# Sums of squares of a feed-forward block by one-column matrix products, later parking of recurrent weights, and other tile sizes

## The chip, the cores and the metric

The kernel runs on one core of one Trainium2 chip. The metric is the device time of one execution in microseconds (us); before the change its median over 3 runs is 2185.7 us (2184.69 to 2186.59). Engines: TensorE (PE; its weight loads PEld), VectorE (DVE), ScalarE (ACT), GpSimd (POOL) and SyncE (SP, whose queue issues the DMAs).

## The reference

A trunk of two decoder layers on an input of 512 rows (S) by 1024 features (D), all in float32. Each layer is a half feed-forward block, a mixer, and another half feed-forward block. The mixer of the first layer is attention (stick-breaking heads and dilated windows), that of the second a recurrent time mixing (RWKV-7). The change is about the four feed-forward blocks:

```python
def rms_norm(x, g, eps=NORM_EPS):
    y = x * lax.rsqrt(jnp.mean(x * x, axis=-1, keepdims=True) + eps)
    return y * g

def swiglu(h, w_gate, w_up, w_down):          # 1024 -> 2816 -> 1024
    return (jax.nn.silu(h @ w_gate) * (h @ w_up)) @ w_down

x = x + 0.5 * swiglu(rms_norm(x, ffn_norm), w_gate, w_up, w_down)
```

## The kernel before

**Stages.** The program has six stages in a row: feed-forward block 0, attention, blocks 1 and 2, the recurrence (rwkv), block 3. x stays in SBUF, features on the partitions, as eight chunks of 128x512. A float32 product is made of three: each operand is split into a high part (a CAST on ACT) and a low part (a subtract on VectorE), and `mm3` (L121 by its matmuls) adds high x high, high x low and low x high in PSUM. A matmul has a 128x128 stationary block and 512 moving columns.

**A feed-forward block** (`ffn`, L538) goes through steps, one converted weight of 128x1024 each, in the order of `ffn_steps`: four steps "s" (`first`, 24 matmuls each) for the first 256 hidden features, then five tiles of 512 hidden features. In a tile, gate and up products of half-size blocks are combined so that seven products ("1", "2", "6", "7", "5", "3", "4", in two halves of 12 matmuls) do the work of eight. In between stand the transposes of the previous tile's result (`turn`, L683) and its down products (`down`, added to x at L704). The combined inputs come from `prep` (splits of x times the gain, L569 and L570) and `sums` (L578 to L584, split by L330 and L331), held in `xs`. What is called a block's head below is the stretch around steps "s" and products 1 and 2; a tile's step of 24 matmuls is one weight of a product or of a down step.

**The norm.** The mean of squares is needed when the first 256 features go through Silu. `first(3)` squares x in four ACT operations of 128x1024 (L610), each into a room from `work()`, adds the eight chunks up on GpSimd in seven adds (L614), and multiplies the 128x512 sum, four blocks of it stationary, by one column of ones (L616, four matmuls, eight passes on TensorE). Then Ln, Exp, two Newton operations and two more on VectorE give rstd (L441 to L445, L620), four Silu on ACT (L103) and four products on VectorE (L624) the first tile's result `u`; its transposes and everything from product 6 on need these. `work()` hands out four rooms in turn, to sums, squares, gate and up results and the results p, q, v, r of the products; the copy of product 1 into p (L660) takes the room of the third square.

**PSUM** has three pairs of banks for products ("fp") and two single ones ("fd"). Steps "s" hold two pairs until Silu and L624 have read them, product 1 takes the third; product 2 needs a pair that has been read.

**Weights** come by DMA (SyncE) as raw 128x1024 into slots: four constant ones and, inside a block, six `extra` ones in the rooms wx. `_conv` turns a raw one into parts (adds L292 where products combine weights, CAST L295, subtract L296), three weights ahead. The next load into a slot waits for the subtract that last read it (L201).

**Parks.** During blocks 1 and 2 the weights of the recurrence are converted in advance and stored to DRAM ("parked"): `park_some` is called with each weight and at each fifth call takes one of 37 operations; the first two are for the lora matrices, four conversions each (`park_lora`, small pieces on ACT L263 and VectorE L264), the others plain pairs (L241, L242, store L245). They have rooms of their own, praw and pparts.

**Order.** Each engine executes its instructions in program order; that order and the places of tiles in SBUF are chosen at build time by a scheduler from the dependences, so that a change in one place can move instructions elsewhere.

## Time and profile before

| | before |
|---|---|
| median of 3 runs | 2185.7 us (2184.69 to 2186.59) |
| profiled execution: its time, its span | 2183.23 us, 2181.5 us |
| mean granted TensorE clock | 0.968 of full speed |
| TensorE busy | 2033.7 us, 93% |
| VectorE busy | 1593.5 us, 73% |
| ACT busy | 954.9 us, 44% |
| GpSimd busy | 189.7 us, 9% |
| moved by DMA | 282.38 MB, 129 GB/s |

The busy time is the sum of an engine's instructions in one profiled execution; the span is from its first to its last instruction, and the execution's own time lies 1.7 us above it. A clock of 0.5 is 1.2 GHz, 1.0 is 2.4 GHz. In the timelines below a row joins neighbouring instructions of one line, with its start and length and the idle time before it.

### The profile page before, as it was taken

Reading aid. Unit: us, or ns where it says so; the run is one execution under the profiler, and the core shown is the slowest. Engines: PE = TensorE matmul, PEld = TensorE weight load, DVE = VectorE, ACT = ScalarE, POOL = GpSimd, SP = SyncE. Lnnn points to the kernel's source line nnn. Section 1 sums busy time; section 2 is a strip of 40 time slices with the busy share of each in tenths; the row PEclk is TensorE's granted clock in tenths of the full one; section 3 lists DMA queues with packets and bytes.
Section 4 is the critical chain, followed back from the end, with each engine's and each line's share of the span. In section 5 each row is a group of like instructions: output and inputs, shape, how many; then the busy total and the mean of one; then the engine's idle time right before and its main releaser. Section 6 shows DMA issues by size and latency. Waiting matters only on the chain.

```text
span 2181.5 us, 28736 instructions
## 1 busy us (share of the span) xinstructions
PE 2033.7 (93%) x11303; PEld 1625.8 (75%) x11303; DVE 1593.5 (73%) x1958; ACT 954.9 (44%) x1367; POOL 189.7 (9%) x194
## 2 busy tenths in 40 slices
PE   6799999999986999999799999999878898999998
PEld 5688888776874778888678888777556666788887
DVE  7587885557777977887788888556964557787774
ACT  4343443354345534445444445383624424333342
POOL 1100000211003000000200000112321104000000
PEclk9899999999997999999899999999988998999999
DMA  5232332421122475555355575446633332233321
GB/s 175 70 114 87 107 98 69 132 78 49 54 92 93 156 236 203 186 193 179 117 187 177 172 229 185 162 126 212 196 105 90 98 116 92 87 116 116 97 87 39
DMA packets 219294, 282.38 MB, mean 129 GB/s; under 512 B 45395, under 2 KB 135659, under 8 KB 219160
## 3 DMA queue, kind: packets, MB, share of 16 engines
q1 hardware_dynamic: 217048, 278.46, 40.3%
q10 hardware_dynamic: 2112, 2.10, 0.3%
q8 instruction: 89, 1.46, 0.3%
q14 instruction: 45, 0.37, 0.1%
HBM read 227.76 MB, written 54.59 MB: 129 GB/s over the span
## 4 chain that ended last, share of the span: by engine, by line
PE 76%; DVE 11%; ACT 4%; DMA 3%; issue 3%; POOL 2%; SPq 1%; POOLq 0%; DVEq 0%; ACTq 0%
PE fp L121 36%; PE fd L121 17%; PE am L121 6%; PE rm L121 4%; PE rq L121 2%; DVE parts L296 2%; PE wo L121 2%; PE rr L121 2%; PE fd L683 1%; POOL ssum L614 1%; PE rl L121 1%; DVE const L1582 1%; DVE const L1588 1%; ACT parts L295 1%; DMA const<-in_ffn_w_up_dram 1%
## 5 line engine op out<-in xcount | busy, mean ns | idle before, releaser
L121 PE MATMUL fp<-parts,xs 128*128 128x512 f32 x3744 | 909.2, 398 | 40.0 <-ACT wx L660 27.2
L121 PEld LDWEIGHTS fp<-parts,xs 128*128 128x128 f32 x3744 | 708.0, 191 | 190.1 <-ACT wx L660 28.0
L121 PE MATMUL fd<-act,parts 128*128 128x512 f32 x1728 | 410.7, 391 | 5.7 <-DVE act L331 5.5
L121 PEld LDWEIGHTS fd<-act,parts 128*128 128x128 f32 x1728 | 325.5, 189 | 76.6 <-DVE act L331 8.4
L295 ACT CAST parts<-wx 128x1024 fp32r<-128x1024 f32 x220 | 230.3, 1052 | 327.0 <-PE fp L121 212.5
L295 ACT CAST parts<-const 128x1024 fp32r<-128x1024 f32 (+1 forms) x196 | 202.2, 1033 | 320.0 <-PE fp L121 155.8
L296 DVE TENSOR_TENSOR parts<-const,parts 128x1024 fp32r<-128x1024 f32 (+1 forms) x196 | 236.7, 1211 | 107.9 <-ACT parts L295 107.2
L296 DVE TENSOR_TENSOR parts<-wx,parts 128x1024 fp32r<-128x1024 f32 x220 | 266.6, 1222 | 59.2 <-ACT parts L295 58.8
L704 DVE SCALAR_TENSOR_TENSOR const<-fd,const 128x512 f32<-128x512 f32 x160 | 109.3, 688 | 121.5 <-PE fd L121 121.4
L646 DVE TENSOR_TENSOR wx<-fp,wx 128x1024 f32<-128x1024 f32 x140 | 169.0, 1220 | 18.6 <-PE fp L121 18.6
L121 PE MATMUL am<-xg,parts 128*128 128x512 f32 x384 | 99.4, 410 | 0.0
L121 PE MATMUL fp<-act,parts 128*128 128x512 f32 x384 | 92.5, 394 | 1.5 <-ACT act L330 1.5
L121 PEld LDWEIGHTS am<-xg,parts 128*128 128x128 f32 x384 | 71.9, 191 | 25.6 <-issue 9.9
L121 PEld LDWEIGHTS fp<-act,parts 128*128 128x128 f32 x384 | 71.0, 188 | 16.8 <-ACT act L330 2.5
L412 POOL TENSOR_TENSOR ssum<-ssum,sq 128x512 f32<-128x512 f32 x14 | 23.1, 1647 | 642.3 <-ACT sq L411 641.9
L614 POOL TENSOR_TENSOR ssum<-wx 128x512 f32<-128x512 f32 x4 | 25.6, 6396 | 602.5 <-ACT wx L610 602.5
L103 ACT ACTIVATE wx<-wx,const 128x512 f32<-128x512 f32 x80 | 53.5, 717 | 55.7 <-DVE wx L646 55.3
L683 PE MATMUL fd<-const,wx 128*128 128x128 f32 x352 | 60.1, 281 | 18.0 <-DVE wx L624 17.4
L683 PEld LDWEIGHTS fd<-const,wx 128*128 128x128 f32 x352 | 45.6, 144 | 33.0 <-issue 15.9
L330 ACT CAST act<-fd 128x512 fp32r<-128x512 f32 x88 | 47.9, 587 | 33.8 <-PE fd L683 33.4
L331 DVE TENSOR_TENSOR act<-fd,act 128x512 fp32r<-128x512 f32 x88 | 57.7, 687 | 6.1 <-ACT act L330 6.1
L121 PE MATMUL rm<-xm,parts 128*128 128x512 f32 x252 | 60.8, 394 | 0.0
(296 smaller groups left out, 2395.9 us busy)
## 6 DMA issues: line engine op xcount, KB each, us to landing
parts<-pparts SPq DMA_DIRECT2D x68, 512.0 KB
parts<-parts SPq DMA_DIRECT2D x68, 512.0 KB
wx<-in_ffn_w_gate_dram SPq DMA_DIRECT2D x52, 512.0 KB
wx<-in_ffn_w_down_dram SPq DMA_DIRECT2D x52, 512.0 KB
wx<-in_ffn_w_up_dram SPq DMA_DIRECT2D x48, 512.0 KB
const<-in_ffn_w_down_dram SPq DMA_DIRECT2D x36, 512.0 KB
const<-in_ffn_w_up_dram SPq DMA_DIRECT2D x32, 512.0 KB
const<-in_ffn_w_gate_dram SPq DMA_DIRECT2D x28, 512.0 KB
```

The lines of the kernel that those rows point to most:

```text
L103: ins = nc.scalar.activation(out, in_, func, **kw)
L121: return self.pe(self.nc.tensor.matmul(*args, **kw))
L295: self.nc.scalar.copy(hi[:r, :n], raw[:, :n])
L296: self.nc.vector.tensor_tensor(out=lo[:r, :n], in0=raw[:, :n], in1=hi[:r, :n].bitcast(F32), op=ALU.subtract)
L330: self.nc.scalar.copy(hi, t)
L331: self.nc.vector.tensor_tensor(out=lo, in0=t, in1=hi.bitcast(F32), op=ALU.subtract)
L412: nc.gpsimd.tensor_tensor(out=ssum, in0=ssum, in1=sq, op=ALU.add)
L614: nc.gpsimd.tensor_tensor(out=ssum, in0=in0, in1=sq[:, e], op=ALU.add)
L646: add = lambda out, other, ps=ps: nc.vector.tensor_tensor(out=out, in0=ps, in1=other, op=ALU.add)
L683: nc.tensor.transpose(ps[:, b * P : (b + 1) * P], us[n][b][:, f * P : (f + 1) * P], self.ident)
L704: nc.vector.scalar_tensor_tensor(out=self.x[c], in0=ps, scalar=0.5, in1=self.x[c], op0=ALU.mult, op1=ALU.add)
L1582: ins = nc.vector.tensor_tensor(out=pv, in0=L[:, i, j:, None].to_broadcast([P, n, j]), in1=T[:, i : i + 1, :j].to_broadcast([P, n, j]), op ...
```

## The change

Line numbers of the changed program are some five higher: L616 is now among the matmuls of `mm` (L120), L610 is L612, L660 is L665, L683 is L688, L624 is L629, L292, L295 and L296 are L293, L296 and L297, L103 is L102, L264 is L265. The reduce is L623.

1. Squares by TensorE. Each of the four steps "s" squares its two chunks and multiplies each of the eight 128x128 blocks of squares by a column of ones into its own column of a PSUM bank, 32 products of 128x128 by 128x1 in a block (128 in all, 16 before). A reduce on VectorE adds the eight columns of each row block. GpSimd's 28 adds are gone. The bank of the sums, one of two "fd", is held through the four steps.

```diff
 def first(kk):
     if not kk:
+        live["sum"] = self.bank("fd", 2)[:, : 4 * NCH]
...
+    sq, c = work(), 2 * kk
+    nc.scalar.activation(sq, self.x_all[:, c : c + 2], AF.Square)
+    for e in range(2):
+        for b in range(4):
+            col = 4 * (c + e) + b
+            self.mm(
+                live["sum"][:, col : col + 1], sq[:, e, b * P : (b + 1) * P], self.ones[:, 0:1],
+                start=True, stop=True,
+            )
     if kk < 3:
         return
-    ssum, ps = self.row("ssum", 1), self.bank("fd", 2)
-    for c in range(0, NCH, 2):
-        sq = work()
-        nc.scalar.activation(sq, self.x_all[:, c : c + 2], AF.Square)
-        for e in range(2):
-            in0 = ssum if c else sq[:, 0]
-            if c or e:
-                nc.gpsimd.tensor_tensor(out=ssum, in0=in0, in1=sq[:, e], op=ALU.add)
-    for b in range(4):
-        nc.tensor.matmul(
-            ps[:, b : b + 1], ssum[:, b * P : (b + 1) * P], self.ones[:, 0:1], start=True, stop=True
-        )
-    self.rsqrt(rstd, ps[:, :4], 1.0 / D, EPS, scratch)
+    sums_of = live["sum"].rearrange("p (c b) -> p b c", b=4)
+    nc.vector.tensor_reduce(out=total, in_=sums_of, axis=AX.X, op=ALU.add)
+    self.rsqrt(rstd, total, 1.0 / D, EPS, scratch)
```

2. Parks. The count of calls starts anew in each block; only calls 13 to 90 count, and every fourth takes an operation (19 in each of blocks 1 and 2, 38 for 37 operations). The rooms praw and pparts go: the raw weight lies in a room of `wx` and the parts in a pair of `act` rooms.

```diff
-        if self.park_ops and self.park_turn % self.park_every == 0:
+        if self.park_ops and 12 < self.park_turn <= 90 and self.park_turn % self.park_every == 0:
...
-    t.plan_parks(5)
+    t.plan_parks(4)
```

3. Tiles. Rooms are pairs of their own instead of groups; the four first inputs of steps "s" lie in a tile xa of their own, whose other halves lie in xs, so `prep` splits each of the four chunks in two halves of 256; the extra raw slots are five instead of six; some tiles are rounded up to 1024 instead of 512. In the mixers biases, q and k, hidden rows, k, pa and heads are grouped otherwise, with the same operations; the lora weights of the recurrence have four buffers instead of five.

```diff
-        self.conv_ahead = 3
-        XS, WX, AC = MODE
...
+        self.conv_ahead, self.park_turn = 3, 0
+        room = [self.pair("wx", 10) for _ in range(10)]
+        x1 = self.t("xa", [4, 2, 256], 1, F32R)
+        xs = [(self.t("xb", [2, 2, 256], 4, F32R), self.t("xs", [2, 4, 256], 4, F32R)) for _ in range(4)]
+        act_room, pair = [self.pair("act", 4, F32R) for _ in range(4)], self.t("acts", [2, 2, S], 1, F32R)
+        act_room += [pair[:, e] for e in range(2)]
+        self.park_room = room[-5], pair
-        self.extra = [room[i].rearrange("p e s -> p (e s)") for i in range(6)]
+        self.extra = [room[i].rearrange("p e s -> p (e s)") for i in range(5)]
...
-        for z in range(4, 10):
+        for z in range(4, 9):
             self.slot_last[z] = -1
...
         def prep(c):
-            hi, lo = (xs[c % 4][:, e, 0:4:3] if c < 4 else xs[c % 4][:, e, 1:3] for e in range(2))
             x = halves(turned(c) if turned else self.x[c])
...
+            if c < 4:
+                parts = [((x1[:, c, 0], x1[:, c, 1]), x[:, 0]), ((xs[c][1][:, 0, 0], xs[c][1][:, 1, 0]), x[:, 1])]
+            else:
+                parts = [((xs[c - 4][0][:, 0], xs[c - 4][0][:, 1]), x)]
...
-            t = act_room[next(turns[6]) % 6]
+            t = act_room[(f + 4) % 6 if n == TILES - 1 else f]
...
-            t = self.t("lw", [2, LORA], 5, F32R)
+            t = self.shaped(self.sb.tile([P, 2 * LORA], F32R, tag="lw", name="lw", bufs=4), [2, LORA])
```

What this does to the engines' orders, at three places (block 3's head, block 1's head, block 1's first tile). On TensorE at the head of block 3 (fp: the products' banks, fd: the single banks; xs, xa and xb: inputs; ssum and wx: the summed squares before, a room with squares now), before:

```order
L121 MATMUL fp<-parts,xs 128x512 x98
L616 MATMUL fd<-const,ssum 128x1 x4
L121 MATMUL fp<-parts,xs 128x512 x24
L683 MATMUL fd<-const,wx_12851 128x128 x6
L121 MATMUL fp<-parts,xs 128x512 x18
L683 MATMUL fd<-const,wx_12851 128x128 x2
```

and now:

```order
L120 MATMUL fp<-parts,xb 128x512 x24
L120 MATMUL fd<-const,wx 128x1 x8
L120 MATMUL fp<-parts,xb 128x512 x24
L120 MATMUL fp<-parts,xa 128x512 x10
L120 MATMUL fd<-const,wx 128x1 x8
L120 MATMUL fp<-parts,xa 128x512 x14
L120 MATMUL fp<-parts,xb 128x512 x24
L688 MATMUL fd<-const,wx 128x128 x6
L120 MATMUL fp<-parts,xs 128x512 x12
```

The four products with ones (L616) stood behind all steps "s" and product 1 and ahead of product 2; now eight stand behind each of the last steps and the last eight inside product 1, and product 2 (the x24 before the transposes L688) has none ahead of it at its start.

On ACT at the head of block 1 (L610 and L612: squares; L660 and L665: the copy of product 1; L263: lora parks), before:

```order
L610 ACTIVATE wx_4147<-const 128x1024
L295 CAST parts<-const 128x1024 x2
L330 CAST xs<-wx_4147 128x1024
L610 ACTIVATE wx_4147<-const 128x1024
L263 ACTIVATE pparts<-praw,const 128x64 x4
L263 ACTIVATE pparts<-praw,const 128x160
L263 ACTIVATE pparts<-praw,const 128x32
L263 ACTIVATE pparts<-praw,const 128x128
L610 ACTIVATE wx_4147<-const 128x1024 x2
L660 COPY wx_4147<-fp 128x1024
```

and now, from the third square on:

```order
L612 ACTIVATE wx<-const 128x1024
L296 CAST parts<-wx 128x1024
L331 CAST xs<-wx 128x1024
L296 CAST parts<-const 128x1024
L665 COPY wx<-fp 128x1024
L296 CAST parts<-const 128x1024
L102 ACTIVATE const<-const 128x4 x2
L98 ACT_TABLE_LOAD
L296 CAST parts<-const 128x1024
L296 CAST parts<-wx 128x1024
L102 ACTIVATE wx<-fp,const 128x256 x4
```

The lora pieces are gone from between the squares and the copy; Ln and Exp (L102 on 128x4), the table load and two CASTs of weights stand ahead of the four Silu (L102 on 128x256).

On VectorE at the same place (L441 to L620, now L442 to L625: rstd from the sums; L624 and L629: the first tile's result), before:

```order
L296 TENSOR_TENSOR parts<-const,parts 128x1024
L441 SCALAR_TENSOR_TENSOR const<-fd,const 128x4
L442 SCALAR_TENSOR_TENSOR const<-const 128x4
L445 SCALAR_TENSOR_TENSOR const<-const 128x4
L620 TENSOR_SCALAR const<-const 128x4
L296 TENSOR_TENSOR parts<-wx_4146,parts 128x1024
L624 SCALAR_TENSOR_TENSOR wx_4147<-fp,const,wx_4147 128x256 x4
```

and now:

```order
L623 TENSOR_REDUCE const<-fd 128x4
L297 TENSOR_TENSOR parts<-const,parts 128x1024
L442 SCALAR_TENSOR_TENSOR const<-const 128x4
L293 TENSOR_TENSOR const<-const 128x1024
L293 TENSOR_TENSOR const<-wx,const 128x1024
L443 SCALAR_TENSOR_TENSOR const<-const 128x4
L293 TENSOR_TENSOR wx<-const,wx 128x1024
L446 SCALAR_TENSOR_TENSOR const<-const 128x4
L297 TENSOR_TENSOR parts<-const,parts 128x1024
L625 TENSOR_SCALAR const<-const 128x4
L297 TENSOR_TENSOR parts<-wx,parts 128x1024
L629 SCALAR_TENSOR_TENSOR wx<-fp,const,wx 128x256 x4
```

The four small operations stood side by side; now the reduce stands ahead of them, and three adds of weights (L293) and two subtracts (L297) between.

On VectorE in the first tile of block 1 (L655 and L660: the last operation of products 3 and 4; L331 and L332: splits of a transposed piece; L242 and L264, L265: parks), before:

```order
L292 TENSOR_TENSOR wx_4147<-const,wx_4147 128x1024
L296 TENSOR_TENSOR parts<-const,parts 128x1024
L292 TENSOR_TENSOR const<-const,wx_4146 128x1024
L296 TENSOR_TENSOR parts<-wx_4146,parts 128x1024
L242 TENSOR_TENSOR pparts<-praw,pparts 128x1024
L292 TENSOR_TENSOR const<-wx_4146 128x1024
L296 TENSOR_TENSOR parts<-wx_4146,parts 128x1024
L331 TENSOR_TENSOR act_4149<-fd,act_4149 128x512 x2
```

and now:

```order
L293 TENSOR_TENSOR wx<-wx 128x1024
L297 TENSOR_TENSOR parts<-wx,parts 128x1024 x2
L265 SCALAR_TENSOR_TENSOR acts<-wx,const,acts 128x64 x4
L265 SCALAR_TENSOR_TENSOR acts<-wx,const,acts 128x160
L265 SCALAR_TENSOR_TENSOR acts<-wx,const,acts 128x32
L265 SCALAR_TENSOR_TENSOR acts<-wx,const,acts 128x128
L297 TENSOR_TENSOR parts<-wx,parts 128x1024
L332 TENSOR_TENSOR act<-fd,act 128x512 x2
L293 TENSOR_TENSOR wx<-const,wx 128x1024
L293 TENSOR_TENSOR const<-const,wx 128x1024
L265 SCALAR_TENSOR_TENSOR acts<-wx,const,acts 128x64 x2
L293 TENSOR_TENSOR const<-wx,const 128x1024
```

Where one plain park (L242) stood, a whole lora conversion (the four rows of L265, seven pieces) and the beginning of the next stand now; all eight lora conversions lie in this tile, six of them ahead of the second pair of splits (L332).

## Rows read from the trace of the kernel before

**Rows 1.** Page, part 1: engine, busy us (share of span), instructions.

```profile
PE 2033.7 (93%) x11303; PEld 1625.8 (75%) x11303; DVE 1593.5 (73%) x1958; ACT 954.9 (44%) x1367; POOL 189.7 (9%) x194
```

**Rows 2.** Stretches (us): each engine's busy time, granted clock, DMA share, GB/s.

```profile
100.00:300.00 200.00, 199.14 (x901) 164.44 (x900) 160.81 (x163) 79.12 (x87) 0.00 (x0) 1.00 0.35 106
740.00:780.00 40.00, 32.92 (x139) 25.76 (x138) 34.34 (x40) 19.49 (x28) 0.00 (x0) 0.91 0.59 199
1120.00:1140.00 20.00, 17.89 (x79) 14.15 (x78) 20.00 (x21) 10.60 (x13) 0.00 (x0) 0.91 0.63 209
```

**Rows 3.** Waits: engine, line, awaited, us in all, times, longest.

```profile
ACT wx L660 <- POOL ssum L614: 26.1, 4, 7.9
```

**Rows 4.** Timeline, TensorE, four block heads: start, us, instructions [idle before].

```profile
63.95 7.03 PE L121 MATMUL fp<-parts,xs 128*128 128x512 f32 x22 [12.53 <-ACT wx L660]
...
78.16 2.05 PE L121 MATMUL fp<-parts,xs 128*128 128x512 f32 x4
...
686.84 7.85 PE L121 MATMUL fp<-parts,xs 128*128 128x512 f32 x22 [14.64 <-ACT wx L660]
694.52 0.95 PE L616 MATMUL fd<-const,ssum 128*128 128x1 f32 x8
...
703.18 1.11 PE L683 MATMUL fd<-const,wx 128*128 128x128 f32 x4 [0.28 <-DVE wx L624]
703.95 2.33 PE L121 MATMUL fp<-parts,xs 128*128 128x512 f32 x5
...
1066.93 1.87 PE L616 MATMUL fd<-const,ssum 128*128 128x1 f32 x8 [7.75 <-POOL ssum L614]
...
1075.62 2.73 PE L121 MATMUL fp<-parts,xs 128*128 128x512 f32 x6
...
1845.85 1.87 PE L616 MATMUL fd<-const,ssum 128*128 128x1 f32 x8 [8.95 <-POOL ssum L614]
...
1858.96 3.59 PE L121 MATMUL fp<-parts,xs 128*128 128x512 f32 x9
```

**Rows 5.** Timeline, GpSimd, block 1's head.

```profile
679.48 9.91 POOL L614 TENSOR_TENSOR ssum<-ssum,wx 128x512 f32<-128x512 f32 x6
```

**Rows 6.** Timeline, ACT, heads of blocks 0 and 1.

```profile
55.49 2.00 ACT L610 ACTIVATE wx<-const 128x1024 f32<-128x1024 f32 x2
...
675.94 1.88 ACT L263 ACTIVATE pparts<-praw,const 128x64 fp32r<-128x64 f32 x7
677.72 1.99 ACT L610 ACTIVATE wx<-const 128x1024 f32<-128x1024 f32 x2
685.77 1.01 ACT L660 COPY wx<-fp 128x1024 f32<-128x1024 f32 x1 [6.07 <-POOL ssum L614]
...
697.60 0.26 ACT L103 ACTIVATE const<-fd,const 128x4 f32<-128x4 f32 x1
...
698.11 1.28 ACT L99 ACT_TABLE_LOAD   x1
...
700.36 0.83 ACT L103 ACTIVATE wx<-fp,const 128x256 f32<-128x256 f32 x2
```

**Rows 7.** Timeline, VectorE, head of block 0 and first tile of block 1.

```profile
56.88 2.17 DVE L292 TENSOR_TENSOR wx<-const,wx 128x1024 f32<-128x1024 f32 x1
...
75.83 0.87 DVE L624 SCALAR_TENSOR_TENSOR wx<-fp,const,wx 128x256 f32<-128x256 f32 x2
...
736.96 1.60 DVE L264 SCALAR_TENSOR_TENSOR pparts<-praw,const,pparts 128x64 fp32r<-128x64 f32 x7
...
747.76 1.22 DVE L292 TENSOR_TENSOR const<-const 128x1024 f32<-128x1024 f32 x1
```

**Rows 8.** Waits of SyncE's DMA queue.

```profile
SPq L201 <- DVE parts L296: 1047.8, 224, 33.3
SPq L245 <- DVE pparts L242: 172.2, 33, 16.7
```

More of the change, by code (lines that the diff above doesn't have):

```diff
@@ L129, in t @@
         n = math.prod(shape)
-        t = self.sb.tile([P, -(-n // S) * S], dtype, tag=tag, name=tag, bufs=bufs)[:, :n]
+        unit = 2 * S if tag in ("vecs", "ssum", "rstd", "recur") else S
+        t = self.sb.tile([P, -(-n // unit) * unit], dtype, tag=tag, name=tag, bufs=bufs)[:, :n]
         return self.shaped(t, shape)
@@ L495, in plan_ffn @@
         for z in steps:
-            i, every = at[z], range(10)
+            i, every = at[z], range(9)
             if z[0] == "s":
@@ L584, in sums @@
             stt(out=t[:, 3], in0=t[:, 1], scalar=-1.0, in1=y12, op0=ALU.mult, op1=ALU.subtract)
-            self.split(t, xs[k][:, 0, 3:7], xs[k][:, 1, 3:7])
+            self.split(t, xs[k][1][:, 0], xs[k][1][:, 1])
         def x_part(k, block, b):
-            return tuple(xs[k][:, e, block, b * P : (b + 1) * P] for e in range(2))
+            bs = slice(b * P, (b + 1) * P)
+            if not block:
+                return tuple(x1[:, k, e, bs] for e in range(2))
+            t, i = (xs[k][0], block - 1) if block < 3 else (xs[k][1], block - 3)
+            return tuple(t[:, e, i, bs] for e in range(2))
         def first(kk):
             if not kk:
+                live["sum"] = self.bank("fd", 2)[:, : 4 * NCH]
                 live["s"] = [t[:, e] for t in (self.banks2(), self.banks2()) for e in range(2)]
@@ L794, in attn_tables @@
         self.bias = []
+        rooms = [self.t(f"bias{g}", [8, P]) for g in range(2)]
         for g, (off, n, kw) in enumerate(((0, 384, 256), (384, 256, P), (640, 256, P))):
@@ L845, in project_v @@
                     f(b, ps[:, i * 256 : (i + 1) * 256], st["rcol"][:, c : c + 1])
-        qkv = self.t("sb", [3, 2, S])
-        qs, ks, vs = qkv[:, 0], qkv[:, 1], qkv[:, 2].rearrange("p i s -> p (i s)")
+        qs, ks, vs = (self.pair("sb", 3) for _ in range(3))
+        vs = vs.rearrange("p i s -> p (i s)")
         for i in range(4):
@@ L889, in attn @@
             merge(out)
-        qk = {}
+        qk, room = {}, [None]
         def evac_norm(ps, g, which):
-            t = all_qk[:, 2 * g + which, :]
+            if not which:
+                room[0] = self.pair("dqk", 6)
+            t, work = room[0][:, which], self.pair("dsq")
+            sq, y = work[:, 0], work[:, 1]
             nc.vector.tensor_tensor(out=t, in0=ps, in1=st["rstd"], op=ALU.mult)
-            sq = self.row("dsq")
             nc.scalar.activation(sq, t, AF.Square)
@@ L1265, in plane @@
     def plane(self, sg, j, i):
-        return self.rw["heads", sg][:, 4 * j + i if i < 4 else 16 + j].rearrange("p c t -> p (c t)")
+        t = self.rw["heads", sg][:, 4 * j + i] if i < 4 else self.rw["us", sg][:, j]
+        return t.rearrange("p c t -> p (c t)")
     def head_keep(self, n, sg, y):
         plane, r = self.heads_at[n, sg]
-        self.split(y, *(self.hids[r + 32 * e : r + 32 * e + 8, plane, :] for e in range(2)))
+        self.split(y, *(self.hid(plane)[r + 32 * e : r + 32 * e + 8] for e in range(2)))
     def head_spread(self, n, m):
@@ L1321, in evac_k @@
         def evac_k(half, ps):
-            all4 = self.t("k", [4, S], 2)
             for i in range(4):
-                t = k_t[4 * half + i] = all4[:, i, :]
+                if i == 0 and not half:
+                    k_t.append(self.t("k", [8, S]))
+                t = k_t[4 * half + i] = k_t[-1][:, 4 * half + i]
                 nc.scalar.copy(t, ps[i])
@@ L1598, in rw_inverse @@
             nc.sync.dma_start(t0[lo], src)
-        us = rw["heads", sg][:, 16:]
+        us = rw["us", sg]
         for s in (1, 0):
```

71 lines of the change are left out of this document (30 added, 41 removed).

## The prediction

> **What bounds the kernel now.** I read the page first: TensorE is busy 93% of the span and VectorE 73% [rows 1]. So only time in which TensorE stands still, or runs slow, can be won. The table of stretches then shows where that is. In the middle of a block it is nowhere: 100 to 300 us is 199.1 us busy at a granted clock of 1.00, 901 matmuls, 0.221 us each, with VectorE at 80% [rows 2]. The waits name the cause: the COPY of product 1 (L660) waits 26.1 us, four times, for GpSimd's sums of squares (L614) [rows 3]. The four block heads on TensorE's timeline show it in place [rows 4]: idle 12.53 us in block 0 and 14.64 in block 1, both released by that COPY, 7.75 in block 2 and 8.95 in block 3, both released by the sums themselves, 43.9 together. The reader should see in each the stretch from the end of product 1 to the start of product 6 (the row after the transposes):
>
> - block 0: 51.42 (63.95 less 12.53) to 78.16, 26.7 us
> - block 1: 672.20 to 703.95, 31.8 us
> - block 2: from 1059.18, with 22 matmuls of product 2 already done (a free PSUM pair let them go ahead), to 1075.62, 16.4 us
> - block 3: 1836.90 to 1858.96, 22.1 us
>
> TensorE needs of this only 24 x 0.221 = 5.3 us for product 2, 0.95 for eight passes with ones [rows 4] and about 1.1 for six transposes (four took 1.11, and the next matmul begins inside them): 7.4 us, in block 2 2.5 us. So 19 + 24 + 14 + 15 = 72 us are lost at the heads, against a whole idle share of some 148 us. Part of it is slow clock: the eight passes took 0.95 us in block 1 and 1.87 us in blocks 2 and 3, right after a wait; the 22 matmuls after block 1's wait took 7.85 us where 4.9 is their pace [rows 4].
>
> **GpSimd's sum goes.** Seven adds on GpSimd per block; in block 1 the last six took 9.91 us, up to 689.4 [rows 5]. The COPY of product 1, whose room held the third square, waited for them and ended at 686.8 [rows 6]. Afterwards a square is read by eight one-column matmuls and is free. All 28 adds go. VectorE gains a little besides: an add (L292) that took 2.17 us while GpSimd ran is elsewhere 1.22 [rows 7].
>
> **128 small matmuls instead of 16.** Each is two passes. The row of eight passes gives 0.95/8 = 0.119 us a pass at full clock, 0.234 at the lower level [rows 4]. Per block 28 more matmuls are 56 x 0.119 = 6.7 us, 27 us in all; that is the bill if TensorE has nothing to wait for, 52 us if all ran at the low clock, nothing if all fill idle time. In blocks 0 and 1 TensorE waits in the first products for VectorE and ACT anyhow, so I let the first 24 be free there and charge only the last eight (1.9 us). In blocks 2 and 3 product 1 runs without gaps up to its end, so 24 x 0.238 = 5.7 us are charged before it. The Trainium skill (TensorE: Matmul & The Clock Gate, section "Wait — 56ns, not 53.3ns?") states that start-to-start never drops below about 25 ns however small the matmul: by that floor the eight would cost 0.4 us and the 24 before them 1.2, and the time would be 4 x 1.5 + 2 x 4.5 = 15 us lower than I give, 2132. The rows show a pass nearly five times as dear, and the rows decide.
>
> **What stays behind the last square.** VectorE's reduce of 128x32 is not in the trace: not below nothing, and not above the 0.44 of a 128x256 operation (half of the pair of L624 in [rows 7]); I take 0.2, since it is an eighth as long. Then Ln and Exp, 0.51 from the one's start to the table load's, the table load 1.28, two pairs of Silu 0.83 each [rows 6], the last L624 0.44 [rows 7], six transposes 1.1: 5.2 us. In the order of the change two CASTs of 128x1024 stand between table load and Silu, each as the COPY 1.01 [rows 6], so 7.2. In block 1 three adds (L293) stand on VectorE inside the chain, between the small operations, 3 x 1.22 = 3.7 us more [rows 7]: 10.9. Product 2's 5.3 us lie inside that. Now the start of product 6, block by block:
>
> - block 0: the last square ended at 57.5 on ACT; 57.5 [rows 6] + 1.9 + 5.2 to 7.2 = 64.6 to 66.6, I take 65.6 against 78.16: 12.6 us won.
> - block 1: the last square ended at 679.7 [rows 6]; one lora conversion (1.88 us on ACT) stood before it and is moved away, so 677.8 + 1.9 + 10.9 = 690.6 against 703.95: 13.4 won.
> - block 2: product 1 ended about 1059.2 - 4.9 = 1054.3; + 5.7 + 1.9 + 7.2 = 1069.1; I take 1069.6 against 1075.62: 6 won.
> - block 3: 1836.9 + 5.7 + 1.9 + 7.2 = 1851.7; the COPY of product 1 now stands behind Exp and the table load, so product 2 starts some 1.3 us late but still ends in time; 1852 against 1858.96: 7 won.
>
> Together 39.0 us.
>
> **The parks, moved.** Before, lora conversions (1.88 us of ACT [rows 6], 1.60 for seven eighths of the same on VectorE [rows 7]) lay in block 1's head and first tile. Now none starts before the 13th weight of a block, and all eight fall into the first tile of block 1, where VectorE was already the bound: 740 to 780 us has it busy 34.3 of 40 us and TensorE 32.9 [rows 2]. Six of them come before the second pair of transposed splits where four and two plain parks were: 1.4 us more by the difference, 5 us if none finds a hole. I charge 3.5. In block 2 the reverse: 1120 to 1140 had VectorE busy 20.0 of 20 us [rows 2]; fewer parks fall there, 2 to 4 us back, I take 3. Net 0.5 lost.
>
> **Other sizes.** In each block four inputs are split in halves, four more operations on each of ACT and VectorE, 16 in all. One cannot cost more than a 128x256 row, 0.44 [rows 7], nor less than nothing: 0 to 7 us on each engine, under ACT's and VectorE's waits for the input at a block's start. I take zero, and 7 us if that cover is gone. The rounding and the pairs move tiles only; the instructions on them stay, and I put them at zero, with plus or minus 5 us for attention and rwkv, whose order on TensorE hardly moves. A raw slot is lost: see the rival.
>
> **Sum.** 39.0 - 0.5 = 38.5. The profiled execution took 2183.2 us (span 2181.5) and the runs' median is 2185.7, 2.5 above. So 2183.2 - 38.5 + 2.5 = **2147 us**. A measurement here can tell about 0.2%, 4.4 us.
>
> **Rivals.**
> 1. *The small matmuls lie on the path everywhere.* The first 24 in blocks 0 and 1 cost 11.4 us more, and if the last eight and half of the rest ran at the low clock another 4 x 3 us: 2147 + 23 = 2170. For it: clock low after each wait [rows 4]. Against: those heads wait for ACT and VectorE, not TensorE. Chance 0.15.
> 2. *Slower: weights come late.* Raw slots fall from ten to nine per block, and for two loads in each tile (the second half of product 6 and the second down step) the distance from the freeing of a slot to its next use falls from three steps to two, 24 x 0.221 = 5.3 us a step. SyncE's queue issues loads in order and waits already: 1047.8 us, 224 times, longest 33.3, for the subtract that frees a slot, and 172.2 us, longest 16.7, in front of a park's store [rows 8]; parks now stand closer, every fourth weight. 512 KB at the 209 GB/s of [rows 2] are 2.5 us. Two such loads in a row, with two conversions of 1.01 + 1.22 us and, by my estimate, 3.5 us of queueing, must fit in four steps, 21.2 us: 5 + 4.5 + 3.5 does. It decides from a landing of about 6.6 us. Then 40 loads are late by 1.5 to 3 us: 60 to 120 us, less 38.5, so 2207 to 2267. Only two of the four blocks hold parks; if only those are hit (20 loads), 2177 to 2207. Against it: mid-block losses are nil with a lead of three steps. Chance 0.15, of which 0.11 slower and 0.04 within 0.2%.
> 3. *VectorE takes over in block 1.* All eight lora conversions in one VectorE-bound tile and the reduce's chain queued behind adds in every block: the 1.5 us not yet charged there, and 3.7 us in the three other heads: 2147 + 13 = 2160. Chance 0.15.
> 4. *All 128 are hidden and the clock stays up.* No charge for small matmuls in blocks 2 and 3: 2147 - 11 = 2136, with the five microseconds of other stages 2131. Chance 0.1.
>
> **How the numbers follow.** The forecast has 0.45, on its own 2137 to 2157. The range takes in rivals 1, 3 and 4: 2131 to 2174; beyond it lie rival 2 and little else, less than 0.2. Faster 0.85 (forecast and rivals 1, 3, 4), same 0.04, slower 0.11.
>
> **What would show it.** Right: GpSimd's adds gone; no wait of L665 for GpSimd; product 6 near 66, 691, 1070 and 1852, each less what was won before it (so near 66, 678, 1047 and 1820); 0.119 us a pass; TensorE's idle time down by some 40 us while its busy time rises. Rival 1: busy time up by over 20 us with clock low at the heads. Rival 2: TensorE waiting for CASTs (L296) that wait for loads in mid-tile, over 1 us, at the same two steps of each tile. Rival 3: idle time before matmuls released by VectorE in block 1's first tile above 10 us. I am wrong if a head keeps a gap over 8 us, or if attention or rwkv moves by more than 5.

## The result and the profile after

The changed kernel takes 2153.96 us (median of 4 runs, 2152.94 to 2157.91) beside 2185.19 of the kernel before on the same chip: ratio 0.9861, 95% interval 0.9844 to 0.9878, 31 us less. The forecast was 2147, with a range of 2131 to 2174. The profiled execution has a span of 2152.0 us, 29.5 less than before, at a mean clock of 0.980 (0.968 before).

The page's first part, engine by engine (busy, share, instructions):

```profile
PE 2054.0 (95%) x11527; PEld 1648.2 (77%) x11527; DVE 1586.2 (74%) x1978; ACT 957.1 (44%) x1383; POOL 126.7 (6%) x166
```

Against [rows 1] TensorE is busy 20.3 us more, VectorE 7.3 less, GpSimd 63 less. So TensorE's idle time fell by 50 us, of which 20 went into more busy time: 112 more small products, 224 passes.

The four heads on TensorE's timeline (start, length, instructions, idle before), as in [rows 4]:

```profile
56.39 1.84 PE L120 MATMUL fd<-const,wx 128*128 128x1 f32 x16
61.99 6.84 PE L120 MATMUL fp<-parts,xb 128*128 128x512 f32 x21 [3.77 <-ACT wx L665]
...
70.24 1.98 PE L120 MATMUL fp<-parts,xs 128*128 128x512 f32 x8
...
674.97 1.84 PE L120 MATMUL fd<-const,wx 128*128 128x1 f32 x16
676.67 5.75 PE L120 MATMUL fp<-parts,xb 128*128 128x512 f32 x24
685.29 0.41 PE L688 MATMUL fd<-const,wx 128*128 128x128 f32 x2 [2.88 <-DVE wx L629]
...
686.64 3.84 PE L120 MATMUL fp<-parts,xs 128*128 128x512 f32 x9
...
1038.84 1.84 PE L120 MATMUL fd<-const,wx 128*128 128x1 f32 x16
...
1052.50 3.11 PE L120 MATMUL fp<-parts,xs 128*128 128x512 f32 x13
...
1817.88 1.84 PE L120 MATMUL fd<-const,wx 128*128 128x1 f32 x16
...
1824.16 5.74 PE L120 MATMUL fp<-parts,xb 128*128 128x512 f32 x24 [1.10 <-ACT wx L665]
...
1830.31 3.00 PE L120 MATMUL fp<-parts,xs 128*128 128x512 f32 x12
```

The four long gaps are gone or small: 12.53 us became 3.77 in block 0, 14.64 became 2.88 (behind product 2, not ahead of it), 7.75 and 8.95 became none and 1.10. A run of 16 passes (records of a one-column product on TensorE, two for each product) took 1.84 us in every head, 0.115 a pass, with the clock up. One run is another matter: in block 1 those of the first two steps "s" stand back to back, 32 passes, and the granted clock falls to 0.5 inside it without a wait, so that the run and the 21 large products behind it are slow:

```profile
650.64 4.75 PE L120 MATMUL fd<-const,wx 128*128 128x1 f32 x32
...
655.25 7.15 PE L120 MATMUL fp<-parts,xb 128*128 128x512 f32 x21
```

The large products, down products among them, are as many as before, so the start of the n-th of a block can be compared in both traces (us; product 1 begins with the 97th, product 6 with the 145th). The last column counts from the end of the block before, so that a mixer in between is included:

| | before | after | difference | won |
|---|---|---|---|---|
| block 0, product 1 | 41.5 | 48.6 | +7.1 | |
| block 0, product 6 | 78.2 | 70.2 | -7.9 | |
| block 0, 241st large product | 101.8 | 92.0 | -9.8 | |
| block 0, last product | 391.3 | 385.1 | -6.2 | 6.2 |
| block 1, first product | 639.4 | 633.6 | -5.7 | |
| block 1, product 1 | 666.6 | 669.5 | +2.9 | |
| block 1, product 6 | 703.9 | 686.6 | -17.3 | |
| block 1, last product | 1026.6 | 1010.6 | -16.0 | 9.8 |
| block 2, product 1 | 1048.6 | 1038.2 | -10.4 | |
| block 2, product 6 | 1075.6 | 1052.5 | -23.1 | |
| block 2, last product | 1391.3 | 1368.6 | -22.7 | 6.7 |
| block 3, product 1 | 1831.3 | 1815.6 | -15.7 | |
| block 3, product 6 | 1859.0 | 1830.3 | -28.6 | |
| block 3, last product | 2174.0 | 2144.5 | -29.5 | 6.8 |

Attention and the recurrence win or lose next to nothing (from block 0's end to block 1's start -6.2 to -5.7, from block 2's end to block 3's start -22.7 to -24.0). In every block the steps ahead of product 1 became longer, by 5.6 to 8.6 us, and what follows it up to product 6 shorter by 13 to 20. The 48 passes ahead of product 1 are 5.5 us at 0.115; the rest of the lengthening is 3 us in block 1, where the clock fell, and 1.9 and 2.8 in blocks 0 and 3, where e1 below, without the passes, is 1.3 and 2.7 longer as well.

### The profile page after: what moved, and what is told of

Read it like the earlier page. It is cut to its first block, busy times and chain, and to the rows that moved or that the text cites. A ratio compares the mean times of both kernels' runs of the same rounds, so it can differ in the third digit from the quotient of the medians.

```text
span 2152.0 us, 29193 instructions
## 1 busy us (share of the span) xinstructions
PE 2054.0 (95%) x11527; PEld 1648.2 (77%) x11527; DVE 1586.2 (74%) x1978; ACT 957.1 (44%) x1383; POOL 126.7 (6%) x166
## 4 chain that ended last, share of the span: by engine, by line
PE 76%; DVE 11%; DMA 5%; ACT 3%; issue 3%; SPq 1%; POOL 0%; ACTq 0%; DVEq 0%; POOLq 0%
PE fp L120 36%; PE fd L120 17%; PE am L120 7%; PE rm L120 4%; DVE parts L297 2%; PE rq L120 2%; PE wo L120 2%; PE rr L120 1%; PE rl L120 1%; DVE const L1593 1%; DMA const<-in_ffn_w_up_dram 1%; DVE const L1599 1%; DVE wx L293 1%; ACT parts L296 1%; DMA wx<-in_ffn_w_up_dram 1%
## 5 line engine op out<-in xcount | busy, mean ns | idle before, releaser
L120 PE MATMUL fp<-parts,xs 128*128 128x512 f32 x2016 | 494.2, 395 | 12.2 <-DVE parts L297 6.4
L120 PEld LDWEIGHTS fp<-parts,xs 128*128 128x128 f32 x2016 | 379.4, 189 | 96.0 <-DVE parts L297 9.7
L120 PE MATMUL fd<-act,parts 128*128 128x512 f32 x1728 | 409.0, 390 | 2.2 <-DVE acts L332 1.6
L296 ACT CAST parts<-wx 128x1024 fp32r<-128x1024 f32 x224 | 234.1, 1052 | 347.0 <-PE fp L120 167.3
L120 PEld LDWEIGHTS fd<-act,parts 128*128 128x128 f32 x1728 | 324.2, 188 | 72.4 <-DVE acts L332 3.4
L297 DVE TENSOR_TENSOR parts<-wx,parts 128x1024 fp32r<-128x1024 f32 x224 | 272.6, 1222 | 76.0 <-ACT parts L296 75.7
L296 ACT CAST parts<-const 128x1024 fp32r<-128x1024 f32 (+1 forms) x192 | 198.3, 1033 | 268.6 <-PE fp L120 135.4
L120 PE MATMUL fp<-parts,xb 128*128 128x512 f32 x1152 | 291.3, 401 | 8.7 <-ACT wx L665 4.9
L297 DVE TENSOR_TENSOR parts<-const,parts 128x1024 fp32r<-128x1024 f32 (+1 forms) x192 | 230.0, 1199 | 73.3 <-ACT parts L296 68.3
L120 PEld LDWEIGHTS fp<-parts,xb 128*128 128x128 f32 x1152 | 216.8, 191 | 55.3 <-ACT wx L665 5.4
L120 PE MATMUL fp<-parts,xa 128*128 128x512 f32 x576 | 141.8, 395 | 2.1 <-ACT xa L569 2.1
L120 PEld LDWEIGHTS fp<-parts,xa 128*128 128x128 f32 x576 | 108.6, 190 | 25.7 <-ACT xa L569 2.5
L120 PE MATMUL am<-xg,parts 128*128 128x512 f32 x384 | 99.5, 411 | 0.0
L120 PEld LDWEIGHTS am<-xg,parts 128*128 128x128 f32 x384 | 72.0, 191 | 25.5 <-issue 10.1
L102 ACT ACTIVATE wx<-wx,const 128x512 f32<-128x512 f32 x80 | 53.5, 717 | 43.1 <-DVE wx L651 42.7
L242 ACT CAST acts<-wx 128x1024 fp32r<-128x1024 f32 (+2 forms) x37 | 37.1, 1003 | 63.3 <-DMA wx<-in_rw_wk_dram 19.1
L120 PE MATMUL rm<-xm,parts 128*128 128x512 f32 x252 | 60.9, 395 | 0.0
L331 ACT CAST act<-fd 128x512 fp32r<-128x512 f32 x80 | 43.6, 587 | 35.3 <-PE fd L688 35.2
L243 DVE TENSOR_TENSOR acts<-wx,acts 128x1024 fp32r<-128x1024 f32 (+2 forms) x37 | 43.1, 1164 | 20.1 <-ACT acts L242 20.0
```

Source lines behind the costliest of these rows:

```text
L102: ins = nc.scalar.activation(out, in_, func, **kw)
L120: return self.pe(self.nc.tensor.matmul(*args, **kw))
L242: nc.scalar.copy(hi, src)
L243: nc.vector.tensor_tensor(out=lo, in0=src, in1=hi.bitcast(F32), op=ALU.subtract)
L296: self.nc.scalar.copy(hi[:r, :n], raw[:, :n])
L297: self.nc.vector.tensor_tensor(out=lo[:r, :n], in0=raw[:, :n], in1=hi[:r, :n].bitcast(F32), op=ALU.subtract)
```

## The experiments

Each kernel ran beside the kernel before on its chip; kernels on different chips are compared by their ratios to it, and a difference in us is that of the ratios times 2183. The changed kernel stands at 0.9861.

Theory A: the gain is the squares' way off GpSimd, and nothing else. Theory B: the later parks carry a part. Theory C: the tile sizes do. Four kernels take parts of the change away or double one.

**e1, all but the squares.**

```diff
-            nc.vector.tensor_reduce(out=total, in_=sums_of, axis=AX.X, op=ALU.add)
...
+                        nc.gpsimd.tensor_tensor(out=ssum, in0=in0, in1=sq[:, e], op=ALU.add)
...
+                nc.tensor.matmul(
+                    ps[:, b : b + 1], ssum[:, b * P : (b + 1) * P], self.ones[:, 0:1], start=True, stop=True
+                )
```

> The changed kernel with the squares summed on GpSimd again (seven adds and four one-column products per block, as before); parks and tile sizes stay changed. Theory A (the gain is the squares' way off GpSimd): about 2185 us, within 5 of the kernel before, and the gaps of TensorE at the four heads are back (over 7 us each, released by the copy of product 1 or by the sums). Theory B (the later parks carry a good part of the gain): 2165 to 2175. Theory C (tile sizes and places carry it): also 2165 to 2175, and the run with sizes alone is then faster than before as well.

Measured: 2187.12 us, ratio to before 1.0026 (1.0013 to 1.0040). The gaps are back, in block 2 half as long as before and in block 1 longer (17.06 us); here on TensorE's timeline in blocks 0, 2 and 3:

```profile
63.92 7.43 PE L120 MATMUL fp<-parts,xb 128*128 128x512 f32 x22 [13.37 <-ACT wx L665]
...
1063.85 1.05 PE L621 MATMUL fd<-const,ssum 128*128 128x1 f32 x8 [3.77 <-POOL ssum L619]
...
1850.65 6.71 PE L120 MATMUL fp<-parts,xb 128*128 128x512 f32 x22 [9.84 <-ACT wx L665]
```

Without the squares nothing is left of the gain; what the other two parts do together costs some 6 us. The squares are worth 36 us. Theory A holds; as sources of the whole gain B and C fall. The edit moves two things at once, the sum from GpSimd to TensorE and the squares from the last step "s" to all four; early squares with GpSimd's sum kept were not run.

**e2, the old rule for parks in the changed kernel.**

```diff
-        if self.park_ops and 12 < self.park_turn <= 90 and self.park_turn % self.park_every == 0:
+        if self.park_ops and self.park_turn % self.park_every == 0:
...
-        self.conv_ahead, self.park_turn = 3, 0
+        self.conv_ahead = 3
...
-    t.plan_parks(4)
+    t.plan_parks(5)
```

> The changed kernel with the old rule for parks: every fifth call from the start of block 1, no window; the rooms they use stay the changed ones. Theory A: 2154 to 2162; the lora conversions lie in the head of block 1 again, which loses 2 to 6 us there, and block 1's first tile and the later tiles of block 2 get 1 to 4 us back. Theory B: 2165 or more. If the closer parks cost more than they win: under 2152.

Measured: 2156.93, ratio 0.9888 (0.9873 to 0.9903), 6 us over the changed kernel (3 by the medians; the two intervals overlap). In e2 and e3 one park falls into block 1's last tile, where its room still holds a transposed piece, so that two down steps compute with other values; the work is the same. Counted between the same products, block 1 ends as in the changed kernel (-16.6 against -16.0) and block 2 as well (-22.1 against -22.7). The difference stands at the end of the recurrence (its last products -17.3 against -20.8). The rule is worth 3 to 6 us, at the edge of what the runs can tell, and not where the forecast looked for it.

**e3, the tile sizes alone** (squares as in e1, parks as in e2).

> Only the tile sizes, rooms, halves of the first inputs and the nine instead of ten raw slots are changed; squares on GpSimd and the old rule for parks. Theory A (sizes are worth nothing): 2181 to 2189. Theory C (sizes win): under 2180. The forecast's rival of late weights (nine slots): over 2190, with waits of TensorE for weights in the middle of the tiles.

Measured: 2191.80, ratio 1.0050 (1.0031 to 1.0070): 9 to 11 us slower. None of it is lost in the middle of block 0's tiles: its last product starts 1.0 us late, product 6 was 0.6 late. It is lost in heads: in block 1 product 2 starts 11.6 us late (1.1 at the block's start), of which 5.4 are left at the block's end (the recurrence takes them back), and in block 3 product 6 comes 4.4 us later than at the block's start. In block 1 the copy of product 1 stands behind a lora conversion on ACT, which waits for the store of the one before it:

```profile
695.62 1.88 ACT L264 ACTIVATE acts<-wx,const 128x64 fp32r<-128x64 f32 x7 [6.35 <-DMA lora<-acts]
```

So the sizes cost about 11 with the old rule, the new rule gives 5 of them back (e3 to e1), and the squares win 36 (e1 to the change) or 35 (e3 to e2). The 5 are at the edge: the intervals of e3 and e1 overlap, and in the two profiled executions 0.7 of them are left (spans of 2187.9 and 2187.2 us), since in e3 the recurrence takes back what block 1's head lost.

**e4, each one-column product twice.**

```diff
                 for b in range(4):
                     col = 4 * (c + e) + b
-                    self.mm(
...
+                    for _ in range(2):
+                        self.mm(
...
```

> The changed kernel with each of its 128 one-column products issued twice in a row, the second with the same result as the first: 32 more per block, 7.6 us of TensorE at 0.119 us a pass and two passes each, 30.5 in all. If they lie on the path in every block: 2180 to 2187. As the forecast charged them (the first 24 free in blocks 0 and 1): 2154 + 4 x 1.9 + 2 x 5.7 = 2173. If they fill idle time: within 4 of 2154. Stage by stage, the distance from the first matmul of a block to product 6 shows it.

Measured: 2201.28, ratio 1.0074 (1.0048 to 1.0101), 46 us over the changed kernel. They lie on the path in all four blocks, but 46 is half as much again as the passes at full clock. TensorE's timeline at the head of block 2, where the changed kernel had its clock at 1.00 throughout (its stretch first, columns as in [rows 2], where the granted clock is the third figure from the end; then e4):

```profile
1010.00:1055.00 45.00, 44.56 (x233) 37.70 (x232) 35.86 (x53) 26.70 (x36) 0.00 (x0) 1.00 0.20 71
```

```profile
1031.11 3.63 PE L120 MATMUL fd<-const,wx 128*128 128x1 f32 x32
...
1040.18 3.83 PE L120 MATMUL fd<-const,wx 128*128 128x1 f32 x32
1043.87 7.13 PE L120 MATMUL fp<-parts,xb 128*128 128x512 f32 x24
1050.84 4.21 PE L120 MATMUL fd<-const,wx 128*128 128x1 f32 x32
1054.91 8.37 PE L120 MATMUL fp<-parts,xb 128*128 128x512 f32 x24
```

Runs of 32 passes now take 3.63 us and more, and the 24 products behind them 7.13 and 8.37 us where 5.75 is their pace. No wait stands ahead of any of them. The stretch of this head is busy without a gap, at a mean clock of 0.88:

```profile
1025.00:1080.00 55.00, 55.00 (x284) 47.34 (x283) 33.08 (x49) 24.96 (x34) 0.00 (x0) 0.88 0.16 57
```

**e8, the same doubled products in runs half as long**, to see whether the length of the run lowers the clock (the lines that these replace are left out).

```diff
...
                 if k >= 4:
                     sums(k - 4)
+                if k % 2 == 0:
+                    sq = work()
+                    nc.scalar.activation(sq, self.x_all[:, k : k + 2], AF.Square)
+                for b in range(4):
+                    for _ in range(2):
+                        self.mm(
+                            live["sum"][:, 4 * k + b : 4 * k + b + 1], sq[:, k % 2, b * P : (b + 1) * P],
+                            self.ones[:, 0:1], start=True, stop=True,
+                        )
...
```

> As e4, each of the 128 one-column products twice, but the 16 products of a step in two groups of 8 (four blocks, twice), each group behind the 12 large products of its own chunk. e4 took 47 us for 128 more products, of which the passes at full clock explain 30: there a run of 32 passes lasted 3.6 us and the granted clock fell to 0.5 within or right after it, with no wait before. Theory (the clock falls because such a run keeps TensorE's array nearly idle): with runs of 16 passes the clock of block 2's head stays at 1.00 and product 6 of block 2 comes 6 us earlier, counted from the block's start, than in e4; time 2180 to 2190. Rival (the doubled products cost more for another reason, as writing the same column twice): as e4, 2198 to 2204.

Measured: 2184.42, ratio 1.0008 (0.9996 to 1.0019), 32 us over the changed kernel, close to the passes alone (30). In block 2's head 12 or 24 large products stand between runs of 1.84 us, and they keep their pace:

```profile
1026.73 1.84 PE L120 MATMUL fd<-const,wx 128*128 128x1 f32 x16
...
1037.56 3.03 PE L120 MATMUL fp<-parts,xb 128*128 128x512 f32 x12
...
1054.13 1.84 PE L120 MATMUL fd<-const,wx 128*128 128x1 f32 x16
1055.83 5.75 PE L120 MATMUL fp<-parts,xa 128*128 128x512 f32 x24
```

The clock of the stretch is 1.00:

```profile
1019.00:1068.00 49.00, 48.70 (x282) 42.13 (x281) 32.81 (x49) 24.89 (x34) 0.00 (x0) 1.00 0.18 62
```

The head of block 2 is 5.6 us shorter than in e4 (from the block's first product to product 6). In block 1 the runs of e8 are not short: 64 passes stand in a row, and there the clock falls as in e4:

```profile
644.67 9.49 PE L120 MATMUL fd<-const,wx 128*128 128x1 f32 x64
```

So the fall of the clock goes with the longer run; writing a column twice cost nothing beyond its passes. The Trainium skill (TensorE: Matmul & The Clock Gate, section "What's actually happening") says that the clock is set by how busy TensorE has been recently. The profile's busy time does not tell it here: in e4's stretch it is 55.00 of 55.00 us at a mean clock of 0.88, so a TensorE that issues one-column products without a break can be granted 1.2 GHz.

**e5, one pass instead of two.** If the passes are on the path, halving them must win.

```diff
-        self.parts_all = self.cp.tile([P, 8192], F32R, name="parts")
+        self.parts_all = self.cp.tile([P, 8194], F32R, name="parts")
...
+        self.one_r = self.parts_all[:, 8192:8194]
+        nc.scalar.copy(self.one_r, self.ones[:, 0:2])
...
-            sq, c = work(), 2 * kk
+            sq, c = act_room[kk], 2 * kk
...
-                        live["sum"][:, col : col + 1], sq[:, e, b * P : (b + 1) * P], self.ones[:, 0:1],
+                        live["sum"][:, 2 * col : 2 * col + 2], sq[:, e, b * P : (b + 1) * P], self.one_r,
```

> The changed kernel with the squares written in the fast float32 form that takes one pass on TensorE instead of two (into act rooms), the moving column doubled to two equal ones: the same 128 products, one pass each, squares rounded a little more. A group of 16 passes took 1.84 us, so 8 passes save 0.92 us a group, 3.7 a block. Theory A (the small products lie on the path in every block): 14.7 us less, 2137 to 2142. The forecast's split (24 of them free in blocks 0 and 1): 4 x 0.9 + 2 x 2.8 = 9.2 less, 2144 to 2147. If they are hidden: within 4 of 2154.

Measured: 2164.14, ratio 0.9915 (0.9900 to 0.9929), 12 us slower than the changed kernel. The expectation missed altogether, and not at the heads: product 6 of block 0 comes 1.7 us earlier than in the changed kernel, and then every tile of the block loses some 1.6 us. In the middle of block 0, with TensorE busy without a gap at full clock, the stretch 180 to 340 us of the changed kernel and of e5:

```profile
180.00:340.00 160.00, 160.00 (x731) 132.77 (x730) 124.29 (x125) 64.82 (x72) 0.00 (x0) 1.00 0.35 105
```

```profile
180.00:340.00 160.00, 160.00 (x713) 129.29 (x712) 119.74 (x122) 62.07 (x71) 0.00 (x0) 1.00 0.35 106
```

731 instructions in 160 us became 713. New there, beside the one-pass form, were the place of the squares, and two columns more in the tile of converted weights, which is laid out ahead of the work tiles.

**e9, the two columns alone**, unused; the order on TensorE, ACT and VectorE is row for row that of the changed kernel, but for two neighbouring small products of the recurrence.

```diff
-        self.parts_all = self.cp.tile([P, 8192], F32R, name="parts")
+        self.parts_all = self.cp.tile([P, 8194], F32R, name="parts")
```

> The changed kernel with two unused columns (8 bytes on each partition) added to the tile of converted weights, so that every tile placed behind it lies 8 bytes further on; the order on every engine is the same, row for row. In e5 and e7, which had such two columns, the middle of a block ran 713 large products in 160 us instead of 731. Theory (the place of tiles off a 64-byte step slows each product by 2.5%): the same 713 in 160 us, and the time 15 to 30 us over the changed kernel's, 2169 to 2184. Rival (the slower pace came from the squares' other form or from the order): within 4 of 2154.

Measured: 2181.32, ratio 0.9995 (0.9984 to 1.0005): 29 us over the changed kernel, the whole gain but a us or two, from eight bytes. The same stretch:

```profile
180.00:340.00 160.00, 160.00 (x713) 129.30 (x712) 122.83 (x125) 62.55 (x70) 0.00 (x0) 1.00 0.34 105
```

The trace also tells which products slow down. Those with one operand in the tile of converted weights (parts) and the other in a work tile (xs, xa, xb, act, xm) start 227 ns apart in the changed kernel and 234 in e9 (medians, the same in block products and down products, where parts changes sides between moving and stationary). Those with both operands in work tiles, xg and lw at the start of the recurrence, keep their pace. Changed kernel, then e9:

```profile
1368.81 13.87 PE L120 MATMUL rl<-xg,lw 128*128 128x512 f32 x60
...
1397.08 19.20 PE L120 MATMUL rm<-xm,parts 128*128 128x512 f32 x84
```

```profile
1387.54 13.87 PE L120 MATMUL rl<-xg,lw 128*128 128x512 f32 x60
...
1415.84 19.77 PE L120 MATMUL rm<-xm,parts 128*128 128x512 f32 x84
```

e5 has the same 13.87 and 19.77. So what slows a product here is, as far as these rows show, not the place of one of its tiles by itself but that of its two operands to each other. The addresses stand in no trace; that all work tiles moved by the same eight bytes is read from the kernel.

**e10, one pass with 64 columns more instead of two** (the edit against e5).

```diff
-        self.parts_all = self.cp.tile([P, 8194], F32R, name="parts")
+        self.parts_all = self.cp.tile([P, 8256], F32R, name="parts")
```

> e5 again with the tile of converted weights longer by 64 columns (256 bytes) instead of 2, so that what lies behind keeps a 64-byte step. If the place of tiles took e5's gain: 731 products in 160 us again, and the gain that e5 was run for, 2137 to 2146. If the squares in act rooms or the other order took it: 2155 or more.

Measured: 2132.65 (2127.09 to 2138.36), ratio 0.9783 (0.9766 to 0.9800), 17 us under the changed kernel (21 by the medians). The pace of the middle is back, and a run of eight one-pass products takes 0.95 us:

```profile
180.00:340.00 160.00, 160.00 (x728) 132.73 (x727) 125.19 (x126) 63.78 (x70) 0.00 (x0) 1.00 0.35 109
```

```profile
1005.21 0.95 PE L122 MATMUL fd<-parts,act 128*128 128x2 f32 x8
```

16 runs shorter by 0.89 us are 14 us; product 1 of block 0 starts 2.5 us earlier than in the changed kernel, that of block 1 4.9 us earlier counted from the block's start, where the clock no longer falls. The rest lies in the mixers (attention runs from -12.7 to -16.2 against before, the recurrence from -42.8 to -47.4), whose order and places moved as well; what the passes caused of it was not separated.

**e6, the copy of product 1 ahead of Ln on ACT**, in all blocks.

```diff
-        self.act(t, src, AF.Ln, scale=scale, bias=self.const(eps)[: t.shape[0]])
+        self.after(self.act(t, src, AF.Ln, scale=scale, bias=self.const(eps)[: t.shape[0]]), dep)
...
-                nc.scalar.copy(p, ps)
+                copy = nc.scalar.copy(p, ps)
+                if n == 0:
+                    live.pop("rest")(copy)
```

> The changed kernel with the copy of product 1 ordered ahead of Ln, Exp and the table load on ACT. Theory A (product 2 stood behind that chain in blocks 0 and 3): the gap of 3.8 us before product 2 in block 0 shrinks to 1 to 1.5, with 1.5 us of low clock behind it gone, and 1.1 us in block 3: product 6 of block 0 starts 3 to 4 us earlier. In time 2149 to 2153: VectorE is busy without a break in block 0's first tile and can take all of block 0's share back, which leaves about 1 us (block 3).

Measured: 2161.95, ratio 0.9910 (0.9895 to 0.9924), 11 us slower than the changed kernel. Block 0 won 3.1 us more than in the changed kernel, although its product 6 came no earlier (70.4). But block 2, where Ln stood ahead of product 1's end, won 0.7 instead of 6.7, and block 3 with the recurrence 0.4 instead of 6.8. The wait put into those two blocks cost more than the one taken away.

**e7, e5 and e6 together.**

> The edits of e5 and e6 together. Theory A: the sum of the two, 2134 to 2141. If the order moved elsewhere decides, more than either alone.

Measured: 2179.72, ratio 0.9982 (0.9971 to 0.9993): the losses of both, for the reasons above.

**e11, the copy first in block 0 alone.**

> e6 with the copy of product 1 put ahead of Ln in block 0 alone; in e6 block 0 won 3.1 us more than in the changed kernel, while blocks 2 and 3, where Ln had stood ahead of the end of product 1, lost 6 each. Expected: block 0 as in e6 and the others as in the changed kernel, 2149 to 2153. If the order elsewhere is reshuffled: up to 2160.

Measured: 2146.47, ratio 0.9839 (0.9824 to 0.9853), 5 us under the changed kernel (7.5 by the medians; the intervals overlap). Block 0 wins 10.0 instead of 6.2, blocks 1 and 2 win 0.7 and 1.4 less, and the recurrence with block 3 10.9 instead of 6.8; its order is the scheduler's and changed too, and the edit is not shown to be the cause of that.

**e12, e10 and e11 together.**

> e10 and e11 together: 2133 to 2143 if both hold and add up; 2145 or more if block 0's VectorE takes one of them back or the order is reshuffled.

Measured: 2131.87 (2130.74 to 2135.17), ratio 0.9773 (0.9759 to 0.9788): the fastest, though not apart from e10. The two edits do not add up: with one-pass sums block 0 already wins 12.7 in e10 and 12.3 here.

## Why the prediction held, and where it did not

**What bounds the kernel: right.** The heads held the time, and the cause was the way of the squares over GpSimd, for which the copy of product 1 and the products with ones waited. e1 shows it by itself.

**The heads' sum, 39.0: a little high; the squares measured 35 to 36.** With the parks the forecast gave the blocks 12.6, 9.9, 9 and 7; the traces show 6.2, 9.8, 6.7 and 6.8, the cost of the sizes among it. The sign that the forecast gave, product 6 near 66, 678, 1047 and 1820, was missed by 4 to 10 us each time (70.2, 686.6, 1052.5, 1830.3), though no head keeps a gap over 8 us and no mixer moved by more than 5.

- *Block 0 failed, in two steps.* "I let the first 24 be free there" was wrong. The 97th product starts 7.1 us later than before, and in e4, with twice the passes, 15.1: they are on the path here too. And "product 2's 5.3 us lie inside" the chain did not hold, because the copy of product 1 stands behind Ln, Exp and the table load on ACT, which the forecast had seen for block 3 alone:

```profile
59.08 0.54 ACT L102 ACTIVATE const<-const 128x4 f32<-128x4 f32 x2 [0.51 <-DVE const L623]
59.63 1.28 ACT L98 ACT_TABLE_LOAD   x1
60.93 1.01 ACT L665 COPY wx<-fp 128x1024 f32<-128x1024 f32 x1
```

  Product 2 waits 3.77 us for it and runs its first products slowly. Last, 9.8 us were won in the first tile (product 3 itself starts 12.5 us earlier, but 12 down products that stood ahead of it now stand behind it) and 6.1 kept in the second: VectorE is busy without a break from 102.8 to 128 us, and TensorE waits for converted weights, with the clock at 0.5 from 127.3 to 130.7. That VectorE is the cause is read from these rows; no run isolates it. The forecast had this limit for block 1 only:

```profile
124.45 0.50 PE L120 MATMUL fp<-parts,xs 128*128 128x512 f32 x1 [0.70 <-ACT parts L296]
126.37 4.60 PE L120 MATMUL fp<-parts,xs 128*128 128x512 f32 x12 [1.41 <-ACT parts L296]
```

- *Block 1 was right as a sum, by two errors that cancel.* The first 24 were not free (8.6 us more ahead of product 1, 3 of them by the low clock), so that 11.6 us were won from the block's start to product 6 where 13.4 was forecast. The chain behind the last square took 9.8 us from the reduce to product 6 (676.84 to 686.64) where 10.9 was priced. With all eight lora conversions in the first tile 1.3 us were lost from product 6 to the block's end (-17.3 to -16.0), not 3.5. The reduce took 0.19 us, 0.2 was taken:

```profile
676.84 0.19 DVE L623 TENSOR_REDUCE const<-fd 128x4 f32<-128x32 f32 x1 [2.08 <-PE fd L120]
```

- *Block 2: 7.1 won at product 6* where 6 was forecast; the 3 us that fewer parks were to give back did not come.
- *Block 3: 7 forecast and 6.8 measured, in part by luck.* 1.3 of the 6.8 come from the recurrence ahead of it; counted from its own start block 3 won 4.6 at product 6 and 5.5 at its end, because 8.3 us were added ahead of product 1 where 5.7 was charged. The gap for the copy was 1.10 us where 1.3 was expected.

**The price of a pass: right,** 0.119 taken, 0.115 measured, between four and five times the floor that a rule had suggested. Another section of the same page of the Trainium skill (TensorE: Matmul & The Clock Gate, section "LDWEIGHTS (loading the stationary operand)") gives the weight load a time of its columns over 1.2 GHz, by estimate 107 ns for 128. The rows at full clock are near it (0.115 us a pass, and a pass with two columns in e10 takes no more, 0.95 us for eight); at the lower clock a pass took 0.234 [rows 4], which that time does not give. That a one-column product costs here the loading of its 128x128 stationary block is likely by this, not shown: no run changed the block.

**The sizes, put at zero: wrong,** 9 to 11 us lost by e3, 6 by e1 with the new rule for parks; this is the term that failed, and its own bound (7 us if the cover is gone, 5 for the mixers) would have held it. Which of the many sizes costs it was not separated. **The parks, 0.5 lost: wrong in sign, as far as the runs can tell,** up to 5 or 6 won by e1, e2 and e3, of which the profiled executions show 0.7 (e3 to e1) and 3.3 (e2 to the change). The two errors go against each other, which is luck and why the total missed by 7 us and not by more.

**The rivals.** Rival 1 (the small products on the path everywhere) was the truer picture: all 128 are on it, by e4, e8 and e10. Its sign came in half: TensorE's busy time rose by 20.3 us, and the granted clock was 0.5 in parts of the heads of blocks 0 and 1, but 1.00 in those of blocks 2 and 3. So its 2170 was too high. Rival 2 (late weights) did not happen: no wait of TensorE in mid-tile repeats from tile to tile, so nine slots suffice here. Rival 3 cost under 2 us in block 1; block 0's second tile had such a stall instead. Rival 4 did not happen.

## What to carry to other kernels

A reduction over the partitions belongs on TensorE when another engine's sum stands between two stretches of matmuls, but its price is the passes, 0.115 us each here, so halve them first: e10 won another 17 us, of which the passes are 14. Spread them, too: 32 in a row cost 3 us of low clock in block 1. When an edit changes a tile's size, compare the pace of an undisturbed stretch (instructions in a fixed window) before reading anything else: eight bytes undid this change's gain. An order forced on all blocks (e6) lost in those that did not need it; forced in block 0 alone (e11) it left blocks 1 and 2 within 1.4 us.

## What the runs showed of the hardware

- With the work tiles moved by 8 bytes against the tile of converted weights, large products with one operand in each ran 2.5% fewer (731 to 713 instructions in 160 us at full clock, 227 to 234 ns from start to start, in e9 with the order kept). Products with both operands in work tiles kept their pace (60 in 13.87 us in both). Moved by 256 bytes (e10) the first kind runs at 227 ns and 728 instructions again. From which step the pace is whole was not tried; the 64 bytes of the expectations are shown by no run.
- One-column products in runs of 32 passes (3.6 us and more) brought the granted clock down to 0.5 without any idle time, in e4 and in block 1 of the changed kernel; in runs of 16 (1.84 us) between large products they did not in the place where e4 did (block 2, e8).
